# A hybrid S5 and RG-LRU block: the LRU stage in program order on three engines, its fill in 48 units of unsplit float32

## The chip, the cores and the metric

The kernel runs on one core of one Trainium2 chip. The metric is device time in microseconds, the median of the runs shown. TensorE (PE in the rows) multiplies, VectorE (DVE), ScalarE (ACT) and GpSimd (POOL) work elementwise, and SyncE (SP) issues the DMAs in one queue.

## What is computed

One layer with 2048 latent tokens and 256 context tokens, 1024 channels, all in float32. The mixer's input projection gives 512 channels to S5 and 512 to the RG-LRU; what follows bears on the change (cut from the reference).

```python
y_s5_lat = s5_glu(ys_lat[0] + ys_lat[1] + ys_lat[2], ...)      # y = gelu(y); y * sigmoid(y @ w_glu + b_glu)
...
xc = centred_depthwise_conv(xr, lru_conv_w, lru_conv_b)        # 4 taps
for d, reverse in enumerate((False, True)):
    r = sigmoid(block_diag(xc, w_rg[d], b_rg[d]))
    i = sigmoid(block_diag(xc, w_ig[d], b_ig[d]))
    log_a = -LRU_C * r * softplus(-lam)
    a, b = exp(log_a), sqrt(-expm1(2 * log_a)) * (i * xc)
    h_d = linear_scan(a, b, h0, reverse)                       # context first, then latent
...
y_lru_lat = from_col_major(h_0 + h_1, rows) * gelu(gr_lat)
out_lat = concatenate([y_s5_lat, y_lru_lat]) @ w_out
x = x + gt1 * rms_norm(out_lat, g_post_mix)                    # then a SwiGLU FFN
```

## The kernel before

`run` calls `front` (norm, input projection, S5 tables), `mix` (S5 scans, with the rest of the input projection as a fill for TensorE), `mix2` and `mix3` (the LRU stage) and `ffn`. The FFN's function begins with the LRU half of the output projection (`tile_out`, L1199 to L1212, tiles `oy`, `ogy`, `fpg`), which reads the S5 half of the output from DRAM (`OSD`) and the gated LRU output (`YLRU`) once all four channel groups are there.

A matrix product is mostly done in three parts: `split` (L59, L62) makes a float32r high part on ScalarE and a float32r low part on VectorE of each operand, and `mm3` (L70 to L72) or `mm3r` (L1028 to L1030) issues three matmuls. S5's own products (L774, L805, L812) and one sum over partitions (L1143) use float32 tiles as they are.

The LRU stage works on four groups `m` of 128 channels, with 2307 columns each (256 context, 3 of padding, 2048 latent). For each group `conv` loads the inputs and the gate weights, runs four passes on VectorE (L921, L923) and splits the result into five pieces of at most 512 columns. For each of two directions, `gates` (L938) computes r and i, 2 x 5 products of three matmuls, with a Sigmoid each, and multiplies i by the conv's result (L941). `decay` (L950, L951, L955, L956) runs Tanh, Exp and two half Squares on ScalarE and two products on VectorE. `scans` (L960, L961, L946) takes a Sqrt on ScalarE, a product and two scans on VectorE. The sum of both directions (L1004) times the gate that is loaded from `GGD` (L1002, L1006) is stored to `YLRU` (L1007). A group's gates are issued inside the iteration of the group ahead of it.

Beside it a fill runs that needs TensorE most: `glu`, eight blocks of 256 columns with 48 matmuls each, and `out_s5`, the S5 half of the output projection, 16 row tiles with two halves of 512 columns and 12 matmuls each; both split their inputs and use PSUM tiles `pgl`. What the fill is worth is written out by hand: the LRU generator yields a number of microseconds owed, and `run` (in `mix`) takes fill steps until it is paid (`DECAY_FILL`, `GATES_FILL`). Only ScalarE's order is the program's own (`manual_schedule`); the order on the other engines and in SP's queue is chosen by the framework's planner. What is left of the fill follows in `mix3`.

Of the kernel before, what the change touches and what calls it, by code (L numbers as in the profile page):

```python
# [18 lines left out]
D = 1024  # L19
# [7 lines left out]
T = 8  # L27
# [18 lines left out]
class Hybrid:  # L46
# [104 lines left out]
    S5_FILL, CONV_FILL, DECAY_FILL, GATES_FILL = 3.9, 0.1, 2.0, (0, 2, 2, 2)  # L151
# [32 lines left out]
    def mix(self):  # L184
# [31 lines left out]
        def rest():  # L216
            with ExitStack() as es:
                yield from self.glu(es)
            with ExitStack() as es:
                yield from self.out_s5(es)  # L220

        fill = rest()
        self.mm = (run, lru, fill, aes, bes)

    def mix2(self):
        run, lru, fill, aes, bes = self.mm

        with self.tc.manual_schedule(engines={self.nc.scalar.engine}):
            run(lru, fill)

    def mix3(self):
        run, lru, fill, aes, bes = self.mm
# [640 lines left out]
    def lru(self, es, bes):  # L873


# [27 lines left out]
        def conv(m):  # L903
# [7 lines left out]
            wh, wl = (p.tile([128, 4, 128], F32R, name=nm, bufs=2) for nm in ("lwh", "lwl"))  # L911
# [5 lines left out]
            self.split(wh, wl, wr)  # L917
# [6 lines left out]
            parts = []  # L924
            for j, (c0, n) in enumerate(CH):
                xh, xl = (p.tile([128, n], F32R, name=f"{nm}{j}") for nm in ("xh", "xl"))
                self.split(xh, xl, xc[:, c0:c0 + n])
                parts.append((xh, xl))
            return wh, wl, parts, xc

        def gates(m, d, wh, wl, parts, xc):
# [16 lines left out]
        def decay(m, d, r):  # L948
            t = pb.tile([128, XO + 1], F32, name="lt")
            nc.scalar.activation(t, r, AF.Tanh, scale=ccol[:, d * 4 + m:d * 4 + m + 1])  # L950
            nc.scalar.activation(r, r, AF.Exp, scale=ncol[:, d * 4 + m:d * 4 + m + 1])  # L951
            for h in halves:
                s = pb.tile([128, H], F32, name="lsq", bufs=2)
                sq = s[:, :h.stop - h.start]
                nc.scalar.activation(sq, r[:, h], AF.Square)  # L955
                v.scalar_tensor_tensor(t[:, h], sq, 1.0, t[:, h], op0=ADD, op1=MUL)  # L956
            return t

        def scans(d, r, i_, t):
            nc.scalar.activation(t, t, AF.Sqrt)  # L960
# [8 lines left out]
        turned = lambda q: q[:, LAT:XO].rearrange("p (c t r) -> p t r c", c=8, t=T)  # L969
        self.wgraw = p2.tile([128, XO + 1], F32, name="xc")[:, :4 * 512].rearrange("p (k f) -> p k f", k=4)  # L970
        nc.sync.dma_start(self.wgraw, A["s5_w_glu"][0].rearrange("(k p) f -> p k f", p=128))
        x = conv(0)
# [3 lines left out]
        yield self.CONV_FILL  # L976
        ri = []
        for d in range(2):
            yield from gates(0, d, *x)
            ri.append(self.rit)  # L980
        for m in range(4):
            ts = [decay(m, d, ri[d][0]) for d in range(2)]
            if m == 3:
# [27 lines left out]
            ri = nxt  # L1011

# [19 lines left out]
    def glu(self, es):  # L1032
# [5 lines left out]
        wg = []  # L1038
        for k in range(4):
            wh, wl = p.tile([128, 512], F32R, name=f"wgh{k}"), p.tile([128, 512], F32R, name=f"wgl{k}")  # L1040
            self.split(wh, wl, self.wgraw[:, k])
            wg.append((wh, wl))
        W = 256

        def load(n):
            y = st.tile([128, 4, W], F32, name="gy", bufs=3)
            nc.sync.dma_start(y, self.YD[:, :, n])
            yh, yl = st.tile([128, 4, W], F32R, name="gyh"), st.tile([128, 4, W], F32R, name="gyl")
            self.split(yh, yl, y)
            return y, yh, yl  # L1050

        def end(n, y, z):
            nc.scalar.activation(z, z, AF.Sigmoid)
            v.tensor_tensor(z, z, y, op=MUL)
            nc.sync.dma_start(self.YS5[:, :, n * W:(n + 1) * W], z)


# [533 lines left out]
```

## Time and profile before

| | us |
|---|---|
| median of 3 runs (lowest, highest) | 2323.95 (2319.48, 2329.18) |
| the profiled execution, its own time | 2329.66 |
| its span, first to last instruction | 2327.9 |
| busy in the span: TensorE | 2101.6 (90%) |
| VectorE | 1714.1 (74%) |
| ScalarE | 994.3 (43%) |
| GpSimd | 808.7 (35%) |
| mean granted TensorE clock | 0.946 |

The busy time of an engine is the sum over its instructions; a busy TensorE is not one at its peak, since matmuls are pipelined and a record overlaps the next. The granted clock is the share of full speed that TensorE's throttle let through: 1.00 is 2.4 GHz, 0.50 is 1.2 GHz, and what lies between is a mean of both. "Idle before" is the time an engine stood still ahead of an instruction, with what ended it. The shares are means over stages with different limits, so a stage is read by its own windows.

### The profile page before, as it was taken

The page shows a single profiled execution, that of the slowest core. Times are in us where ns is not written, and L with a number is a line of the kernel's source. Part 1 is how long each engine was busy: PE and PEld are TensorE (multiplying, and loading weights), DVE is VectorE, ACT ScalarE, POOL GpSimd, SP SyncE. Part 2 cuts the span into 40 slices and gives each one's busy share as a digit, 9 for nine tenths or more (in the row PEclk, how much of TensorE's full clock was granted, in tenths as well). Part 3 has the DMA queues.
Part 4 walks back from the last instruction along what each step waited for, and adds up shares of the span by engine and source line. Part 5 has one row for each costly group of instructions (what it writes and reads, how often), then busy time and mean ns, then how long its engine had stood idle before and what let it go on. Part 6 is the DMA issues. An engine that isn't in the chain of part 4 may idle for free. (4 is left out here: it accounts for less than half of the span.)

```text
span 2327.9 us, 27391 instructions
## 1 busy us (share of the span) xinstructions
PE 2101.6 (90%) x9460; PEld 1662.1 (71%) x9460; DVE 1714.1 (74%) x2243; ACT 994.3 (43%) x1561; POOL 808.7 (35%) x478
## 2 busy tenths in 40 slices
PE   6599998897674899879999999999999999999987
PEld 1477865575564677658888887788888878888866
DVE  6985458999998748956777878977787763534768
ACT  4688412112777626763333334333333333232424
POOL 1431420440000003343335545656565511400682
PEclk8799999898886899889999999999999999999999
DMA  9577756765233377863443334544444375634663
GB/s 261 171 243 255 232 149 211 212 206 171 71 122 115 127 236 251 285 222 108 146 136 127 109 100 141 176 139 160 143 156 145 136 262 172 214 100 157 226 219 121
DMA packets 311627, 403.29 MB, mean 173 GB/s; under 512 B 60176, under 2 KB 222528, under 8 KB 309952
## 3 DMA queue, kind: packets, MB, share of 16 engines
q1 hardware_dynamic: 311360, 401.50, 53.2%
q8 instruction: 75, 1.23, 0.2%
q14 instruction: 64, 0.52, 0.1%
q0 software_dynamic: 128, 0.04, 0.0%
HBM read 269.33 MB, written 132.12 MB: 172 GB/s over the span
## 5 line engine op out<-in xcount | busy, mean ns | idle before, releaser
L70 PE MATMUL fp<-op,fws 128*128 128x512 f32 x1232 | 486.9, 396 | 8.2 <-ACT op L59 7.5
L71 PE MATMUL fp<-op,fws 128*128 128x512 f32 x1232 | 486.4, 395 | 3.6 <-DVE op L62 2.4
L72 PE MATMUL fp<-op,fws 128*128 128x512 f32 x1232 | 485.3, 394 | 0.0
L70 PEld LDWEIGHTS fp<-op,fws 128*128 128x128 f32 x1232 | 233.7, 190 | 62.5 <-ACT op L59 9.1
L71 PEld LDWEIGHTS fp<-op,fws 128*128 128x128 f32 x1232 | 233.0, 189 | 58.9 <-DVE op L62 5.0
L72 PEld LDWEIGHTS fp<-op,fws 128*128 128x128 f32 x1232 | 233.1, 189 | 51.8
L1029 PE MATMUL po<-gw,ga 128*128 128x512 f32 x616 | 241.7, 394 | 9.4 <-DVE gw L62 9.4
L1028 PE MATMUL po<-gw,ga 128*128 128x512 f32 x616 | 241.6, 394 | 4.1 <-ACT ga L59 2.8
L1030 PE MATMUL po<-gw,ga 128*128 128x512 f32 x616 | 237.8, 391 | 1.5 <-DVE ga L62 1.5
L1348 POOL TENSOR_TENSOR fs<-fraw 128x512 f32<-128x512 f32 x44 | 68.4, 1554 | 484.0 <-DMA fraw<-in_w_ffn_in_dram 381.6
L62 DVE TENSOR_TENSOR fws<-fraw,fws 128x512 fp32r<-128x512 f32 x132 | 126.7, 961 | 56.5 <-ACT fws L59 55.6
L59 ACT ACTIVATE fws<-fraw 128x512 fp32r<-128x512 f32 x132 | 82.9, 629 | 147.0 <-PE fp L72 79.2
L1029 PEld LDWEIGHTS po<-gw,ga 128*128 128x128 f32 x616 | 117.2, 190 | 34.5 <-DVE gw L62 10.1
L1028 PEld LDWEIGHTS po<-gw,ga 128*128 128x128 f32 x616 | 117.3, 190 | 29.3 <-ACT ga L59 3.2
L1030 PEld LDWEIGHTS po<-gw,ga 128*128 128x128 f32 x616 | 116.2, 189 | 26.7 <-DVE ga L62 2.4
L62 DVE TENSOR_TENSOR fws<-fs,fws 128x512 fp32r<-128x512 f32 x132 | 118.1, 895 | 8.1 <-ACT fws L59 6.3
L59 ACT ACTIVATE fws<-fs 128x512 fp32r<-128x512 f32 x132 | 82.5, 626 | 93.2 <-PE fp L72 92.2
L62 DVE TENSOR_TENSOR ga<-gys,ga 128x1024 fp32r<-128x1024 f32 (+2 forms) x88 | 113.8, 1299 | 10.8 <-ACT ga L59 10.8
L71 PE MATMUL pu<-ht,winh 128*128 128x512 f32 (+1 forms) x256 | 100.8, 394 | 10.9 <-DVE ht L62 10.9
L70 PE MATMUL pu<-ht,winh 128*128 128x512 f32 (+1 forms) x256 | 102.3, 404 | 6.7 <-ACT ut L416 3.4
L62 DVE TENSOR_TENSOR gw<-gch,gw 128x512 fp32r<-128x512 f32 x44 | 51.6, 1172 | 71.5 <-ACT gw L59 71.5
L62 DVE TENSOR_TENSOR gw<-graw,gw 128x512 fp32r<-128x512 f32 x44 | 37.1, 843 | 88.7 <-ACT gw L59 85.4
(532 smaller groups left out, 4751.3 us busy)
## 6 DMA issues: line engine op xcount, KB each, us to landing
fraw<-in_w_ffn_in_dram SPq DMA_DIRECT2D x88, 512.0 KB, 4.4
graw<-in_w_ffn_out_dram SPq DMA_DIRECT2D x99, 256.0 KB, 3.6
gys<-S SPq DMA_DIRECT2D x44, 512.0 KB, 4.0
A<-faf SPq DMA_DIRECT2D x33, 512.0 KB, 2.6
S<-ost SPq DMA_DIRECT2D x33, 512.0 KB, 3.0
alw<-in_w_ada_dram SPq DMA_DIRECT2D x24, 512.0 KB, 5.0
ost<-A SPq DMA_DIRECT2D x22, 512.0 KB, 5.1
gys<-A SPq DMA_DIRECT2D x22, 512.0 KB, 5.0
```

The lines of the kernel that those rows point to most:

```text
L59: self.nc.scalar.activation(hi, src, AF.Identity)
L62: (eng or self.nc.vector).tensor_tensor(lo, src, hi.bitcast(F32), op=SUB)
L70: mm(ps, wh, xh, start=first, stop=False)
L71: mm(ps, wh, xl, start=False, stop=False)
L72: mm(ps, wl, xh, start=False, stop=last)
L1028: mm(ps, xh, wh, start=first, stop=False)
L1029: mm(ps, xh, wl, start=False, stop=False)
L1030: mm(ps, xl, wh, start=False, stop=last)
L1348: g.tensor_tensor(s[0], a21, a22, op=ADD)
```

## The change

`mix2` puts TensorE, ScalarE and VectorE in program order for the whole LRU stage. The LRU generator now yields a kind of fill, "g" or "o", and a count of units. A "g" unit is half a GLU block (2 x 4 matmuls of 256 columns into one PSUM tile), an "o" unit is one half of an output row tile (4 matmuls of 512 columns). Both use float32 operands without a split. There are 16 of the one and 32 of the other, 48 in all; four and three "g" units stand ahead of the gates of group 0, then 11 units go with each of groups 0 to 2 and seven with group 3, "g" units only where ScalarE's functions are Sigmoid and Tanh. A unit's eviction from PSUM is issued behind the matmuls of the next unit: two Sigmoids with the bias inside, or one copy, all on ScalarE.

In the LRU code the loads are apart from the conv, `parts` holds the splits and stands between the decay products and the Sqrt, the products of i with the conv's result stand ahead of the next conv, and the gating of a group (`gated`) is put off into the iteration of the next one. The sum of both directions goes into the conv's buffer. The GLU weights and the first four blocks of `w_out` are loaded into tiles of their own when the stage begins; before, the former came ahead of the conv of group 0 and the latter in group 1, and both were split.

```diff
     def mix2(self):
-        run, lru, fill, aes, bes = self.mm
-
-        with self.tc.manual_schedule(engines={self.nc.scalar.engine}):
-            run(lru, fill)
+        lru, aes, bes = self.mm
+        self.fes = ExitStack()
+        fill = {}
+
+
+        nc = self.nc
+        with self.tc.manual_schedule(engines={nc.tensor.engine, nc.scalar.engine, nc.vector.engine}):
+            for kind, n in lru:
+                if not fill:
+                    fill = self.lru_fill(self.fes)
+                for _ in range(n):
+                    next(fill[kind])
+            for f in fill.values():
+                for _ in f:
+                    pass
+            self.evict()
...
         self.wo = self.split_w_out(self.pool(self.wes, "wo_b", 1), self.woraw)
-        for _ in fill:
-            pass
+        self.fes.close()
         bes.close()
...
-        def conv(m):
+        def load(m):
...
-            self.split(wh, wl, wr)
+            return xs, wr
...
+        def parts(wr, xc):
+            wh, wl = (p.tile([128, 4, 128], F32R, name=nm, bufs=2) for nm in ("lwh", "lwl"))
+            self.split(wh, wl, wr)
...
-                yield self.GATES_FILL[m]
-            v.tensor_tensor(ri[1], ri[1], xc, op=MUL)
-            self.rit = ri
+            return ri
...
-            nc.scalar.activation(t, t, AF.Sqrt)
             v.tensor_tensor(i_, i_, t, op=MUL)
...
-        self.wgraw = p2.tile([128, XO + 1], F32, name="xc")[:, :4 * 512].rearrange("p (k f) -> p k f", k=4)
-        nc.sync.dma_start(self.wgraw, A["s5_w_glu"][0].rearrange("(k p) f -> p k f", p=128))
...
+        def gated(m, y, gg):
+            gv = gg.rearrange("p (t r c) -> p t r c", t=T, c=8)
+            v.tensor_tensor(gv, y[:, LAT:XO].rearrange("p (c t r) -> p t r c", c=8, t=T), gv, op=MUL)
+            nc.sync.dma_start(self.YLRU[:, m, :], gg)
...
+        yield "g", 4
+        xs, wr = load(1)
+        ri, old = [gates(0, 0, *x)], None
+        yield "g", 3
+        ri.append(gates(0, 1, *x))
         for m in range(4):
-            ts = [decay(m, d, ri[d][0]) for d in range(2)]
-            if m == 3:
+            for d in range(2):
+                v.tensor_tensor(ri[d][1], ri[d][1], xc, op=MUL)
+            if old:
+                gated(*old)
+            if m < 3:
+                xn = conv(m + 1, xs)
+            else:
 
                 raws = [p2.tile([128, XO + 1], F32, name="xc") for _ in range(2)]
                 self.woraw = [self.raw_w_out(raws[k // 2][:, k % 2 * D:(k % 2 + 1) * D], 4 + k) for k in range(4)]
-            else:
-                x = conv(m + 1)
-            yield self.DECAY_FILL
+            ts = [pb.tile([128, XO + 1], F32, name="lt") for _ in range(2)]
...
             for d in range(2):
-                scans(d, *ri[d], ts[d])
-            if m == 1:
-
-                raws = [ri[1][0][:, k * D:(k + 1) * D] for k in range(2)]
-                raws += [pb.tile([128, H], F32, name="lsq", bufs=2)[:, :D] for k in range(2)]
-                self.woraw = [self.raw_w_out(raws[k], k) for k in range(4)]
+                nc.scalar.activation(ts[d], ri[d][0], AF.Tanh, scale=ccol[:, d * 4 + m:d * 4 + m + 1])
+                if m < 3:
+                    yield "og"[d == 0], 1
+            for d in range(2):
+                r = ri[d][0]
+                nc.scalar.activation(r, r, AF.Exp, scale=ncol[:, d * 4 + m:d * 4 + m + 1])
+                yield "o", 1
+                for h in halves:
+                    s = pb.tile([128, H], F32, name="lsq", bufs=2)
+                    sq = s[:, :h.stop - h.start]
+                    nc.scalar.activation(sq, r[:, h], AF.Square)
+                    v.scalar_tensor_tensor(ts[d][:, h], sq, 1.0, ts[d][:, h], op0=ADD, op1=MUL)
+                yield "o", 1
+            if m < 3:
+                x = parts(wr, xn)
+                yield "o", 1
+            for d in range(2):
+                nc.scalar.activation(ts[d], ts[d], AF.Sqrt)
+                if d == 0 or m == 3:
+                    yield "o", 1
+            if m < 2:
+                xs, wr = load(m + 2)
             nxt = []
             if m < 3:
-                yield from gates(m + 1, 0, *x)
-                nxt.append(self.rit)
+                nxt.append(gates(m + 1, 0, *x))
+            scans(0, *ri[0], ts[0])
+            scans(1, *ri[1], ts[1])
             gg = ri[1][1][:, :SEQ]
             nc.sync.dma_start(gg, self.GGD[m])
-            y = ts[0]
-            v.tensor_tensor(y[:, LAT:XO], y[:, LAT:XO], ts[1][:, LAT:XO], op=ADD)
-            gv = gg.rearrange("p (t r c) -> p t r c", t=T, c=8)
-            v.tensor_tensor(gv, turned(y), gv, op=MUL)
-            nc.sync.dma_start(self.YLRU[:, m, :], gg)
+            y = xc if m < 3 else ts[0]
+            v.tensor_tensor(y[:, LAT:XO], ts[0][:, LAT:XO], ts[1][:, LAT:XO], op=ADD)
+            old = m, y, gg
+            yield ("g", 3) if m < 2 else ("o", 3) if m == 2 else ("o", 1)
             if m < 3:
-                yield from gates(m + 1, 1, *x)
-                nxt.append(self.rit)
+                nxt.append(gates(m + 1, 1, *x))
+                xc = xn
             ri = nxt
+        gated(*old)
...
+        wg = p.tile([128, 4, 512], F32, name="wg")
+        nc.sync.dma_start(wg, A["s5_w_glu"][0].rearrange("(k p) f -> p k f", p=128))
         W = 256
-
-        def load(n):
+        self.evict = lambda: None
+
+        def unit(end):
+            self.evict()
+            self.evict = end
...
+        gy = [load_g(n) for n in range(2)]
+        wo = [self.raw_w_out(p.tile([128, D], F32, name=f"wo{k}"), k) for k in range(4)]
+
+        def glu():
+            for n in range(8):
+                if n < 6:
+                    gy.append(load_g(n + 2))
+                z = st.tile([128, 4, W], F32, name="gz")
+                for m0 in (0, 2):
+                    pg = ps.tile([128, 2, W], F32, name="pgl")
+                    for m in (m0, m0 + 1):
+                        for k in range(4):
+                            nc.tensor.matmul(pg[:, m - m0], wg[:, k, m * 128:(m + 1) * 128], gy[n][:, k],
+                                             start=k == 0, stop=k == 3)
+
+                    def end(n=n, m0=m0, pg=pg, z=z):
+                        for m in (m0, m0 + 1):
+                            nc.scalar.activation(z[:, m], pg[:, m - m0], AF.Sigmoid,
+                                                 bias=self.colsB[:, C_BGLU + m:C_BGLU + m + 1])
+                        if m0:
+                            v.tensor_tensor(z, z, gy[n], op=MUL)
+                            nc.sync.dma_start(self.YS5[:, :, n * W:(n + 1) * W], z)
+
+                    unit(end)
+                    yield
+
+        def out():
+            ys = [load_o(i) for i in range(2)]
+            for i in range(16):
+                if i < 14:
+                    ys.append(load_o(i + 2))
+                o = st.tile([128, D], F32, name="oso")
+                for h in range(2):
+                    cs = slice(h * 512, (h + 1) * 512)
+                    po = ps.tile([128, 512], F32, name="pgl")
+                    for k in range(4):
+                        nc.tensor.matmul(po, ys[i][:, k], wo[k][:, cs], start=k == 0, stop=k == 3)
+
+                    def end(i=i, h=h, o=o, po=po, cs=cs):
+                        nc.scalar.activation(o[:, cs], po, AF.Copy)
+                        if h:
+                            nc.sync.dma_start(self.OSD[i], o)
+
+                    unit(end)
+                    yield
+
+        return {"g": glu(), "o": out()}
```

## Rows read from the trace of the kernel before

**Rows 1.** Stretches: us, busy us (count) by engine, PEclk, DMA share, GB/s.

```profile
577.00:600.00 23.00, 20.59 (x108) 17.92 (x108) 20.68 (x34) 17.18 (x28) 0.33 (x6) 0.88 0.44 149
600.00:665.00 65.00, 40.26 (x233) 35.71 (x234) 61.33 (x48) 43.52 (x49) 0.89 (x6) 0.81 0.30 102
831.00:871.00 40.00, 37.91 (x167) 30.82 (x167) 10.83 (x16) 8.61 (x14) 5.07 (x4) 1.00 0.82 266
```

**Rows 2.** Timeline of ScalarE: start us, us, engine, line, operation, tiles.

```profile
599.35 2.23 ACT L950 ACTIVATE lt<-lr,lc 128x2308 f32<-128x2308 f32 x1
614.40 2.48 ACT L59 ACTIVATE xh<-xc 128x512 fp32r<-128x512 f32 x5
779.78 2.24 ACT L950 ACTIVATE lt<-lr,lc 128x2308 f32<-128x2308 f32 x1
```

**Rows 3.** Timeline of SP's DMA queue, end of the LRU work.

```profile
830.08 0.32 SPq L1007 DMA_DIRECT2D YLRU<-li  x1
839.01 0.53 SPq L1201 DMA_DIRECT2D ogy<-YLRU  x1
```

**Rows 4.** Timeline of TensorE, where the next stage begins.

```profile
870.99 0.39 PE L1028 MATMUL fpg<-woh,oyh 128*128 128x512 f32 x1
871.22 0.39 PE L1029 MATMUL fpg<-wol,oyh 128*128 128x512 f32 x1
```

**Rows 5.** Tile pgl: ns min/median/max, first and last start us.

```profile
L70 PE MATMUL pgl<-gyh,wgh x128: 276/283/583, 577.7 to 719.8; 128*128 128x256 f32 x128
```

**Rows 6.** Groups of VectorE, 566 to 872 us: busy us, mean ns, idle.

```profile
L1073 DVE TENSOR_SCALAR gz<-pgl,colsB 128x256 f32<-128x256 f32 x32 | 14.5, 476 | 2.0 <-PE pgl L72 2.0
L1098 DVE COPY oso<-pgl 128x512 f32<-128x512 f32 x16 | 11.0, 686 | 20.3 <-PE pgl L1030 13.0 <-DMA OSD<-oso 7.3
L62 DVE TENSOR_TENSOR gyl<-gy,gyh 128x1024 fp32r<-128x1024 f32 x8 | 9.8, 1222 | 1.2 <-ACT gyh L59 1.2
L941 DVE TENSOR_TENSOR li<-li,xc 128x2308 f32<-128x2308 f32 x8 | 20.4, 2556 | 5.7 <-ACT li L938 5.7
L1006 DVE TENSOR_TENSOR li<-lt,li 128x2048 f32<-128x2048 f32 x4 | 15.7, 3916 | 1.2 <-DMA li<-GGD 1.2
L921 DVE TENSOR_SCALAR xc<-xs,colsB 128x2307 f32<-128x2307 f32 x4 | 5.9, 1478 | 0.8 <-DMA xs<-XRD 0.7
L923 DVE SCALAR_TENSOR_TENSOR xc<-xs,colsB,xc 128x2307 f32<-128x2307 f32 x12 | 31.4, 2617 | 0.1
L956 DVE SCALAR_TENSOR_TENSOR lt<-lsq,lt 128x1154 f32<-128x1154 f32 x16 | 21.3, 1356 | 13.5 <-ACT lsq L955 13.4
L946 DVE TENSOR_TENSOR_SCAN lt<-lr,lt,li 128x2048 f32<-128x2048 f32 x8 | 35.6, 4466 | 0.0
L1004 DVE TENSOR_TENSOR lt<-lt 128x2048 f32<-128x2048 f32 x4 | 9.1, 2286 | 0.0
```

**Rows 7.** Groups of ScalarE, 566 to 872 us, the same columns.

```profile
L938 ACT ACTIVATE lr<-pg,colsB 128x512 f32<-128x512 f32 x32 | 22.0, 688 | 12.2 <-PE pg L72 12.2
L938 ACT ACTIVATE lr<-pg,colsB 128x260 f32<-128x260 f32 x8 | 3.8, 477 | 4.3 <-PE pg L72 4.3
L955 ACT ACTIVATE lsq<-lr 128x1154 f32<-128x1154 f32 x16 | 17.8, 1157 | 0.2
L960 ACT ACT_TABLE_LOAD x4 | 5.1, 1283 | 0.1
L1101 ACT ACTIVATE oso<-pgl 128x512 f32<-128x512 f32 x16 | 9.5, 596 | 42.3 <-PE pgl L1030 31.9 <-DMA OSD<-oso 10.3
```

**Rows 8.** Timeline of TensorE, runs of float32 matmuls.

```profile
559.10 1.13 PE L805 MATMUL py<-u,md 128*128 128x256 f32 x4
395.79 1.12 PE L1143 MATMUL py<-g,ones 128*128 128x512 f32 x2
```

**Rows 9.** Tile li: loads of GGD, issue to landing.

```profile
DMA to landing us min/median/max: 4.6/4.7/5.1
```

**Rows 10.** Waits of ScalarE, 735 to 872 us: total, times, longest.

```profile
ACT oso L1101 <- PE pgl L1030: 31.9, 9, 7.3
```

More of the change, by code (lines that the diff above doesn't have):

```diff
@@ L214, in mix @@
             next(lru)
[L216 to L223, printed above, removed]
-    def mix2(self):
-        run, lru, fill, aes, bes = self.mm
-        with self.tc.manual_schedule(engines={self.nc.scalar.engine}):
-            run(lru, fill)
+        self.mm = (lru, aes, bes)
+    def mix2(self):
+        lru, aes, bes = self.mm
[12 more added lines that the diff above has]
+            self.evict()
     def mix3(self):
-        run, lru, fill, aes, bes = self.mm
+        lru, aes, bes = self.mm
         aes.close()
         self.wo = self.split_w_out(self.pool(self.wes, "wo_b", 1), self.woraw)
-        for _ in fill:
-            pass
+        self.fes.close()
         bes.close()
@@ L927, in conv, with gates @@
                 self.split(xh, xl, xc[:, c0:c0 + n])
-                parts.append((xh, xl))
-            return wh, wl, parts, xc
-        def gates(m, d, wh, wl, parts, xc):
+                ps_.append((xh, xl))
+            return wh, wl, ps_
+        def gates(m, d, wh, wl, parts):
             ri = [(pb.tile([128, XO + 1], F32, name=nm, bufs=1) if (2 * m + d) % 3 == 2 else
@@ L946, in lru @@
         scan = lambda o, a, b, x0: v.tensor_tensor_scan(o, a, b, x0, op0=MUL, op1=ADD)
[L948 to L957, printed above, removed]
         def scans(d, r, i_, t):
-            nc.scalar.activation(t, t, AF.Sqrt)
             v.tensor_tensor(i_, i_, t, op=MUL)
@@ L967, in scans @@
                 scan(t[:, XO - 1:LAT - 1:-1], r[:, XO - 1:LAT - 1:-1], i_[:, XO - 1:LAT - 1:-1], t[:, 0:1])
-        turned = lambda q: q[:, LAT:XO].rearrange("p (c t r) -> p t r c", c=8, t=T)
-        self.wgraw = p2.tile([128, XO + 1], F32, name="xc")[:, :4 * 512].rearrange("p (k f) -> p k f", k=4)
-        nc.sync.dma_start(self.wgraw, A["s5_w_glu"][0].rearrange("(k p) f -> p k f", p=128))
-        x = conv(0)
+        def gated(m, y, gg):
+            gv = gg.rearrange("p (t r c) -> p t r c", t=T, c=8)
+            v.tensor_tensor(gv, y[:, LAT:XO].rearrange("p (c t r) -> p t r c", c=8, t=T), gv, op=MUL)
+            nc.sync.dma_start(self.YLRU[:, m, :], gg)
+        xs, wr = load(0)
+        xc = conv(0, xs)
+        x = parts(wr, xc)
         yield None
@@ L1046, in load, with load_g @@
+        def unit(end):
+            self.evict()
+            self.evict = end
+        def load_g(n):
             y = st.tile([128, 4, W], F32, name="gy", bufs=3)
             nc.sync.dma_start(y, self.YD[:, :, n])
[L1048 to L1055, printed above, removed]
@@ L1059, in glu @@
-        nxt, last = load(0), None
-        yield 0.1
-        for n in range(8):
-            y, yh, yl = nxt
-            nxt = load(n + 1) if n < 7 else None
-            z = st.tile([128, 4, W], F32, name="gz")
-            for m in range(4):
-                if m % 2 == 0:
-                    pgs = ps.tile([128, 2, W], F32, name="pgl")
-                pg = pgs[:, m % 2]
-                ms = slice(m * 128, (m + 1) * 128)
-                for k in range(4):
-                    self.mm3(pg, wg[k][0][:, ms], wg[k][1][:, ms], yh[:, k], yl[:, k], k == 0, k == 3)
-                b = self.colsB[:, C_BGLU + m:C_BGLU + m + 1]
-                v.tensor_scalar(z[:, m], pg, b, None, op0=ADD)
-            if last:
-                end(*last)
-            last = n, y, z
-            yield 5.2
@@ L1078, in glu @@
-        end(*last)
-    def out_s5(self, es):
-        nc, v = self.nc, self.nc.vector
-        wop = self.pool(es, "wo_a", 1, side="right")
-        p = self.pool(es, "osp", 2, side="right")
-        ps = self.pool(es, "osps", 4, side="right", space=PSUM)
-        wo = self.split_w_out(wop, self.woraw)
-        yield 10.0
-        def load(i):
-            y = p.tile([128, 4, 128], F32, name="osy")
-            nc.sync.dma_start(y, self.YS5[:, :, i * 128:(i + 1) * 128])
-            yh, yl = p.tile([128, 4, 128], F32R, name="osyh"), p.tile([128, 4, 128], F32R, name="osyl")
-            self.split(yh, yl, y)
-            return yh, yl
-        def end(o, i, h, po):
-            cs = slice(h * 512, (h + 1) * 512)
-            if h:
-                v.tensor_copy(o[:, cs], po)
-                nc.sync.dma_start(self.OSD[i], o)
-            else:
-                nc.scalar.activation(o[:, cs], po, AF.Copy)
-        nxt, last = load(0), None
-        for i in range(16):
-            yh, yl = nxt
-            nxt = load(i + 1) if i < 15 else None
-            o = p.tile([128, D], F32, name="oso")
-            for h in range(2):
-                cs = slice(h * 512, (h + 1) * 512)
-                po = ps.tile([128, 512], F32, name="pgl")
-                for k in range(4):
-                    self.mm3r(po, yh[:, k], yl[:, k], wo[k][0][:, cs], wo[k][1][:, cs], k == 0, k == 3)
-                if last:
-                    end(*last)
-                last = o, i, h, po
-                yield 2.6
-        end(*last)
@@ new lines, in load_g, with load_o @@
+            return y
+        def load_o(i):
+            y = st.tile([128, 4, 128], F32, name="osy", bufs=4)
+            nc.sync.dma_start(y, self.YS5[:, :, i * 128:(i + 1) * 128])
+            return y
+        gy = [load_g(n) for n in range(2)]
[20 more added lines that the diff above has]
+                    yield
```

19 lines of the change are left out of this document (5 added, 14 removed).

## The prediction

> **What bounds the kernel now.** I read the stretches of the stage first, then the busy groups of VectorE and ScalarE in it, then four moments in the timelines. The chain that ended last lies wholly behind the stage (it begins at 1876 us), so it says nothing here; what counts is when the next stage, the LRU half of the output with the name fpg, can begin. In [rows 1] VectorE is busy for 61.3 of 65 us in the first whole channel group, while TensorE has 40.3 us and a mean clock of 0.81; after 831 us VectorE has 10.8 of 40 us and TensorE 37.9. So the stage has two parts: up to about 831 us VectorE's work sets the pace, and behind it 40 us in which TensorE only works off what is left of the S5 half of the output. The moments in [rows 2 to 4] give the same: the first tanh of group 0 starts at 599.35, that of group 3 at 779.78, so a group takes 60.1 us; the gated output of group 3 goes to DRAM at 830.08, and fpg starts only at 870.99, right behind the last S5 output. The first GLU matmul started at 577.7 [rows 5].
>
> **What is removed.** On VectorE, the bias adds behind the GLU, 14.5 us, half of the S5 output's copies, 11.0, the low parts of the GLU's input, 9.8 [rows 6], and three smaller kinds of split. ScalarE loses the high parts and takes the bias inside the Sigmoid, 32 of 256 columns (0.48 each, by the 260-column form) and 16 more copies of 0.60 [rows 7]. None of that is added to the sum by itself: it decides which engine is late in the walk below.
>
> **What TensorE pays.** A float32 matmul stands in the trace as two instructions. Four of 256 columns last 1.13 us from the first start to the last end, two of 512 columns 1.12 [rows 8]. A record outlasts the distance to the next start: 0.39 against 0.23 in [rows 4], so 0.16 of each figure is the drain. The first of a run waits 0.11 for its weights (an estimate: 1.13 - 0.16 = 0.97 = 0.11 + 4 x 0.215, and with the same two numbers 2 x 0.43 + 0.11 + 0.16 = 1.13, which the row of 512 columns gives). So a code matmul costs 0.43 at 256 columns, 0.86 at 512; a GLU unit (8 of 256) and an output unit (4 of 512) cost 3.45 each, and 48 units 165 us at full clock. The three-part form at 0.23 a piece would be 12 x 0.23 = 2.8 for an output unit: the change makes TensorE's own work longer by over a fifth. The gates of one direction stay as they are: 24 x 0.23 plus 6 of 260 columns at about half, 6.2 us.
>
> **The start.** The seven GLU units before group 0 are now ahead of its gates, in TensorE's order: 7 x 3.45 + 2 x 6.2 = 36.6. The GLU weights, 1 MB, now ask for their place in SP's queue just ahead of the first GLU input; between nothing (they leave while S5 is still being stored) and 4.7 us (the 1 MB load of GGD, from issue to landing [rows 9]) I take 1.3, so units start at 579. The four w_out blocks, 2 MB, and the next xs follow behind and are needed 40 us later: nothing. The clock was 0.88 in the first 23 us, a quarter of it at 1.2 GHz [rows 1]: 2.5 us lost. With the last Sigmoid, 0.7, the first tanh starts at 579 + 36.6 + 2.5 + 0.7 = 618.8, 19 us later than now.
>
> **The groups.** Per group TensorE has 11 units and two gates, 38 + 12.4 = 50.4. Group 0 takes 52: that, and 1.6 in which the gates wait for ScalarE's table load (1.28 [rows 7]). In groups 1 and 2 VectorE starts with the previous group's output: from the last Sigmoid, 2.56 (li x xc) + 3.92 (gating) + 9.33 (conv, 1.48 + 3 x 2.62) + 1.22 (a GLU product, the size of a split of 1024 columns) = 17.0, and only then the first decay product, 1.36 [rows 6]. ScalarE has its third Square ready to go at 15.7 but both lsq buffers are full until 18.4, and the fourth until 19.7. Behind it: Square to 20.9, the conv splits 3.1 (2.48 for the five pieces [rows 2] and 0.6 for the weights), evictions, table load and Sqrt (the size of the tanh, about 2.1) to 28.6, the second Sqrt 31.3, table load 32.6, ten Sigmoids at TensorE's pace to 38. Then three units, 10.4, and the other gates, 6.2, and a Sigmoid: 55. TensorE idles some 4 us in it. VectorE's two scan rows, 2 x (2.56 + 0.7 + 4.47), and the sum of both, 2.29, run from 28.6 to 46 beside the units: hidden, by 8 us. If the units' cover went, this path would still end before 55. So the groups take 52 + 55 + 55 = 162, and group 3 starts at 780.8, almost where it starts now.
>
> **The end.** Group 3 has no gates and no conv. ScalarE: two tanh 4.4, table 1.3, two Exp 4.4, four Squares 4.6, table 1.3, Sqrt 2.1, some evictions 1.8, about 20.5 with the wait for the last decay product. VectorE: 15.4 for two directions, to 36; the gate's load is issued then and takes 4.7 [rows 9], over the sum's 2.29; gating 3.92: 45. The trace has 50.3 for the same stretch, 779.78 to 830.08, with other work between; these are the bounds. From the store to fpg the load of the stored rows was issued 8.9 later, behind other DMAs [rows 3]; with load and split between 10 and 15, I take 11. TensorE has worked off the units by then, so fpg starts at 780.8 + 56 = 836.8, on a clock that has fallen: 2.5 more. Against 870.99 that is 31.7 us earlier, and the next stage follows as it did.
>
> The profiled execution took 2329.66 us (span 2327.9), 5.7 over the median of the runs: 2329.66 - 31.7 = 2298.0, and from the median, 2323.95 - 31.7 = **2292 us**.
>
> **Costed at nothing.** That y lies in xc, that the load of xs and the gate weights is apart from the conv, and the one unit behind group 3 (its eviction is done long before the gating ends). The input loads of the output units stand two tiles, four units or 14 us, ahead; a 1 MB load takes 4.7 [rows 9], so they cover. If SP holds them behind the load of GGD, which waits for the last scan, the units behind that stop, then the gates of direction 1, then the next tanh. Bounds: 0 and 5 us a group.
>
> **Rivals.**
> A. *The cadence stays.* The units stand in ScalarE's and VectorE's way as the splits did, or SP delays their inputs, and a group takes 60.1 as now [rows 2]. For it: the group's path has only 8 us of slack on VectorE. Against: the work removed from VectorE [rows 6]. Then 618.8 + 180.4 + 56 + 2.5 = 857.7, 13.3 gained: 2311.
> B. *TensorE alone counts.* The wait for the lsq buffers doesn't show and a group takes 50.4: 828.3, or 2281.
> C. *Taking turns, slower than before.* With three engines in program order, a unit's eviction waits in ScalarE's queue for TensorE, and tanh, Exp and Sqrt wait behind it. Place: the seven evictions between tanh and Sqrt. If every unit were waited for, a group would be 38 of units, 24.5 of ScalarE's own functions, 8 of evictions and 13.8 of gates: 84, the start of fpg at 930, the time 2383. It decides from 64.6 a group, (870.99 - 2.5 - 56 - 618.8) / 3, so from a wait of about 1 us at each of 11 units. For it: ScalarE waited 31.9 us for S5 output matmuls in the last third of the stage, in nine waits [rows 10]. Against: the eviction of a unit is issued behind the matmuls of the next, and four banks let TensorE run on; in the walk it is 1.5 to 3 us ahead at each.
> The Trainium skill's page "TensorE: Matmul & The Clock Gate" (Architectural detail) has ScalarE and VectorE as strict FIFOs, and that speaks for C; the nine waits agree with it.
> D. *The clock.* While TensorE had 40 of 65 us to do, its clock was 0.81 [rows 1]. If the idle pieces of the new order held it there, 50.4 would be 62 and a group about 66: 2328, no change. Against: the new groups leave 4 us idle of 55, and at 95% busy the clock was 1.00 [rows 1].
> The Trainium skill's page "TensorE: Matmul & The Clock Gate" (HAM oscillation) says that bursts broken by waits start each time on the slow clock, which speaks against so finely cut an order; by it the time would be D's, by the row of 831 to 871 us the forecast's.
>
> **How the numbers follow.** Chances: the walk 0.61, A 0.14, B 0.09, C 0.08, D 0.08. The range reaches from B with the two cold starts left out and its DMA wait at nothing, 2281 - 5 - 1.3 = 2274, to A with 3 for the weights' load, 2314: what is left out is C and most of D. A measurement of this kernel can tell about 0.5%, 11.6 us, from no change, so faster means under 2312. The walk and B are faster, and 0.09 of A's 0.14: 0.79. The rest of A and D: 0.13. Slower is C: 0.08.
>
> **What would show it.** Right: units of about 3.45 us from first to last start; the first tanh near 619; three distances of 52 to 55 between the tanh of successive groups; third Squares idle behind decay products; fpg near 837, with TensorE idle for some 25 us before it; the stage behind it as long as now. Wrong: tanh of groups 60 apart or more; ScalarE waiting long for pgl; units over 4 us; a stretch in the groups with a clock near 0.8; DMA as what units wait for.

## The result and the profile after

| us | before | after |
|---|---|---|
| median (lowest, highest), 9 runs each | 2320.5 (2312.59, 2330.99) | 2297.74 (2294.23, 2311.28) |
| ratio of the times, 95% interval | | 0.9900 (0.9883 to 0.9916) |
| the profiled execution, its own time | 2329.66 | 2294.62 |
| its span | 2327.9 | 2292.8 |
| mean granted TensorE clock | 0.946 | 0.957 |

The change makes the kernel 1.0% faster, 23 us, with an interval of 19.5 to 27. The prediction put what can be told from no change at 0.5%. The forecast was 2292 in a range of 2274 to 2314.

The two profiled executions differ by 35 us, and that is more than the change is worth. The next stages begin 27 us earlier, as shown below; the rest is the last stage (tile `po`), which took 437 us in the one profile and 428 in the other. In the seven further profiles of this study it took between 428 and 436, whatever was edited in the LRU stage, so nothing ties it to the change.

The busy times of the page show where not to look. Against the table ahead of the prediction, VectorE lost 50 us of work and ScalarE 11, and TensorE gained 8, but the gain can't be read from these sums:

```profile
PE 2109.9 (92%) x9204; PEld 1626.7 (71%) x9204; DVE 1664.5 (73%) x2163; ACT 983.7 (43%) x1569; POOL 811.2 (35%) x478
```

What counts is when the LRU stage ends. These are its stretches in the kernel after, to be held against [rows 1] (us, then busy us and count for TensorE, its weight loads, VectorE, ScalarE and GpSimd, then granted clock, DMA share, GB/s). They are cut at the moments of the new order: seven GLU units and the first gates, the groups 0, 1 and 2, the units beside group 3, the bare end, the next stage.

```profile
579.00:619.00 40.00, 40.00 (x178) 34.34 (x179) 6.92 (x9) 18.88 (x34) 0.00 (x0) 0.95 0.52 167
619.00:669.00 50.00, 50.00 (x181) 33.04 (x180) 42.55 (x26) 41.74 (x55) 0.69 (x4) 1.00 0.43 137
669.00:724.00 55.00, 51.82 (x181) 34.09 (x180) 46.50 (x26) 42.00 (x54) 0.79 (x5) 0.97 0.41 139
724.00:779.00 55.00, 51.81 (x156) 29.32 (x155) 45.44 (x25) 41.68 (x53) 0.10 (x1) 0.97 0.32 110
779.00:807.00 28.00, 27.69 (x64) 11.58 (x62) 20.30 (x13) 27.63 (x27) 0.00 (x0) 1.00 0.47 169
807.00:840.00 33.00, 0.00 (x0) 0.00 (x0) 17.11 (x6) 0.86 (x2) 4.04 (x4) 0.58 0.58 183
840.00:944.00 104.00, 99.38 (x435) 79.54 (x436) 89.52 (x172) 71.13 (x129) 35.38 (x16) 0.94 0.77 260
```

Before, TensorE had 40 of 65 us to do in a group, at a clock of 0.81, and 40 us of leftover work behind the stage. Now it is full in the groups (50 of 50, 52 of 55, clock 0.97 to 1.00), and nothing is left behind group 3: it stands still from 807 to 840, waiting for the LRU output.

The moments, in us, for all kernels of this study ("units": first and last start of their matmuls; tanh: first start in group 0 and in group 3; the three distances are those between the first tanh of successive groups; "store": issue of group 3's store to `YLRU`; `fpg`: first matmul of the next stage; `fp`: first matmul of the FFN behind it):

```
kernel               units          tanh 0  distances          tanh 3  store   fpg    fp
before               577.7 - 870.8  599.4   65.5  61.5  53.5   779.8   830.1   871.0   982.8
after                579.0 - 806.3  618.6   50.2  55.3  55.2   779.3   826.7   840.4   955.8
e5_unsplit_only      576.8 - 872.0  607.8   58.1  56.5  65.0   787.3   837.4   872.1   985.6
e4_fill_last         718.4 - 923.8  588.1   40.2  46.5  46.2   721.0   767.1   923.9  1039.3
e3_two_banks         576.9 - 809.2  616.0   50.6  53.7  53.7   774.0   822.9   836.5   951.9
e1_squares_in_xs     580.8 - 799.2  619.8   50.2  51.1  51.1   772.2   819.6   833.1   947.0
e2_wo_late           573.8 - 800.2  613.2   50.2  55.3  55.2   773.9   818.0   831.6   947.5
e6_shift             578.4 - 818.2  607.1   51.6  55.1  56.4   770.2   819.7   834.5   950.9
e7_all               581.5 - 812.0  611.3   51.5  51.2  51.2   765.1   810.3   826.3   940.5
```

One of the four runs of `e5_unsplit_only` took 9190.55 us, four times the others, and stands in no figure below.

From tanh 0 to tanh 3 a group now takes 53.6 on average instead of 60.1, but the first tanh comes 19 later, so group 3 starts when it did (779.3 against 779.8). The LRU output is stored 3.3 us earlier, no more. The gain is behind it: before, the next stage waited for the units until 871.0; now it starts 13.7 us behind the store.

The timeline of ScalarE shows a group in the kernel after (start us, us, line, operation, tiles, and in brackets the idle time before it with what ended it):

```profile
618.59 2.23 ACT L993 ACTIVATE lt<-lr,lc 128x2308 f32<-128x2308 f32 x1
...
646.80 0.69 ACT L947 ACTIVATE lr<-pg,colsB 128x512 f32<-128x512 f32 x1
...
655.11 0.84 ACT L1094 ACTIVATE gz<-pgl,colsB 128x256 f32<-128x256 f32 x2 [2.25 <-PE pgl L1089]
658.57 0.84 ACT L1094 ACTIVATE gz<-pgl,colsB 128x256 f32<-128x256 f32 x2 [2.62 <-PE pgl L1089]
...
668.80 2.23 ACT L993 ACTIVATE lt<-lr,lc 128x2308 f32<-128x2308 f32 x1
...
687.34 2.38 ACT L1003 ACTIVATE lsq<-lr 128x1154 f32<-128x1154 f32 x2 [3.55 <-DVE lt L1004]
...
699.55 1.28 ACT L947 ACT_TABLE_LOAD   x1
700.84 0.69 ACT L947 ACTIVATE lr<-pg,colsB 128x512 f32<-128x512 f32 x1
...
792.75 2.22 ACT L1003 ACTIVATE lsq<-lr 128x1154 f32<-128x1154 f32 x2
794.86 3.89 ACT L59 ACTIVATE woh<-xc 128x1024 fp32r<-128x1024 f32 x4
...
839.70 0.63 ACT L59 ACTIVATE oyh<-ogy 128x512 fp32r<-128x512 f32 x1 [32.14 <-DMA ogy<-YLRU]
```

Two GLU units are evicted 3.46 us apart: that is the price of a unit. The third and fourth Square of group 1 wait 3.55 for VectorE's decay product. In group 3 four splits of `w_out` stand behind the last Square, 3.89 us, ahead of the Sqrt.

The tile `pgl` in the kernel after (ns min/median/max, first and last start), and at its end who waited for it:

```profile
L1089 PE MATMUL pgl<-gy,wg x256: 377/379/763, 579.0 to 726.5; 128*128 128x256 f32 x128
L1113 PE MATMUL pgl<-wo,osy x256: 592/592/697, 621.2 to 806.3; 128*128 128x512 f32 x128
...
  DVE gz L1097: 27.2, 3
  ACT gz L1094: 18.4, 8
  ACT oso L1116: 5.4, 3
```

ScalarE waited 31.9 us for S5 output matmuls in the last third of the old stage [rows 10]; over the whole of the new one it is 5.4. Its 18.4 for GLU units lie at the start and in the three units at the end of a group, where the walk of the prediction has TensorE set the pace.

### The profile page after: what moved, and what is told of

Read it like the earlier page. It is cut to its first block, busy times and chain, and to the rows that moved or that the text cites. A ratio compares the mean times of both kernels' runs of the same rounds, so it can differ in the third digit from the quotient of the medians.

```text
span 2292.8 us, 26775 instructions
## 1 busy us (share of the span) xinstructions
PE 2109.9 (92%) x9204; PEld 1626.7 (71%) x9204; DVE 1664.5 (73%) x2163; ACT 983.7 (43%) x1569; POOL 811.2 (35%) x478
## 5 line engine op out<-in xcount | busy, mean ns | idle before, releaser
L62 DVE TENSOR_TENSOR ga<-gys,ga 128x1024 fp32r<-128x1024 f32 (+2 forms) x88 | 120.6, 1375 | 14.7 <-ACT ga L59 14.4
L1113 PE MATMUL pgl<-wo,osy 128*128 128x512 f32 x256 | 111.2, 593 | 0.2 <-ACT oso L1116 0.2
L72 PE MATMUL pu<-ht,winl 128*128 128x512 f32 (+1 forms) x256 | 99.6, 389 | 0.0
```

Of the source, the lines that this page charges most:

```text
L62: (eng or self.nc.vector).tensor_tensor(lo, src, hi.bitcast(F32), op=SUB)
L72: mm(ps, wl, xh, start=False, stop=last)
L1113: nc.tensor.matmul(po, ys[i][:, k], wo[k][:, cs], start=k == 0, stop=k == 3)
```

## The experiments

The theory to be tested is the walk of the prediction: the order lets TensorE take the units beside the groups, and a group is then set by single, nameable waits on ScalarE and VectorE. Its rivals were that the units' simpler form alone brought the gain, that the wait for the Square buffers was cover and not path, and that taking turns held the groups at 55. The ratios below set times against the kernel before; the intervals of e1, e2 and e6 overlap with that of the kernel after, so what each of them adds to it is read from the profiles, one execution each.

**e5_unsplit_only: the kernel before, with the operands unsplit.** With the splits their buffers go: the weights are loaded straight into tiles of their own, and the output units' inputs have four buffers instead of two. The order is still the planner's, and the fill steps and evictions stay.

```diff
-            self.split(yh, yl, y)
-            return y, yh, yl
+            return y
...
-                    self.mm3(pg, wg[k][0][:, ms], wg[k][1][:, ms], yh[:, k], yl[:, k], k == 0, k == 3)
+                    nc.tensor.matmul(pg, wg[:, k, ms], y[:, k], start=k == 0, stop=k == 3)
...
-                    self.mm3r(po, yh[:, k], yl[:, k], wo[k][0][:, cs], wo[k][1][:, cs], k == 0, k == 3)
+                    nc.tensor.matmul(po, y[:, k], wo[k][:, cs], start=k == 0, stop=k == 3)
```

> The kernel before with one part of the change alone: GLU and S5 half of the output in float32 matmuls without splits; the order, the steps of the fill and the evictions stay as they were. Theory (the order and the place of the units carry the gain): VectorE loses 28 us of low parts, so the LRU work ends between 803 and 831 us, but about 15 output units are still left then, as in the kernel before, and at 3.45 us instead of 2.72 they take 52 us: fpg begins between 855 and 883, the time is 2310 to 2335, no change or a small gain. Rival (dropping the splits is what gains): fpg near 840 and 2297, as in the changed kernel.

Measured: 2322.48, 2331.6 and 2333.25 us, against a median of 2321.18 of the kernel before on the same chip, ratio 1.005 (1.003 to 1.0071): no gain, and by the median about 0.5% slower, though VectorE has less to do. The LRU work did not end between 803 and 831 as expected, but at 837.4. `fpg` starts 1.1 us later than before; where the rest lies, the profile doesn't show, since it is of the fastest of these runs. Why nothing is gained, it does, in the columns of above:

```profile
600.00:665.00 65.00, 40.95 (x163) 32.26 (x161) 51.35 (x37) 43.02 (x51) 0.79 (x5) 0.79 0.29 98
837.00:872.00 35.00, 30.81 (x71) 13.52 (x72) 6.18 (x9) 4.24 (x7) 4.97 (x4) 1.00 0.78 255
```

VectorE went from 61.3 to 51.4 of 65 us [rows 1], and no engine took the room: TensorE still has 41 us at a clock of 0.79, and still 35 us of units behind the store. Less work on the busiest engine brought nothing while the order stayed the planner's. The other half, the new order with the three-part splits, wasn't tried. So what is shown is that the unsplit form alone does not bring the gain; whether the order alone would is open.

**e4_fill_last: the new order, with all 48 units behind group 3.**

```diff
             for kind, n in lru:
                 if not fill:
                     fill = self.lru_fill(self.fes)
-                for _ in range(n):
-                    next(fill[kind])
```

> The changed kernel with no unit beside the groups: all 48 stand behind group 3. It shows what the LRU chain costs alone. Theory (group 0 is set by TensorE's units, groups 1 and 2 by the chain VectorE - Squares - Sqrt - gates - units - gates): without units a group takes 46 to 48 us, set by VectorE's 45, the first tanh starts near 591, that of group 3 near 731, and fpg comes behind 165 us of units near 905, so the time is about 2360. If the units cost the groups nothing, the groups would stay at 50 and 55 us. If the chain's waits alone set the 55, it would stay for groups 1 and 2.

Measured: 2383.76 us (one run). The bare groups take 40.2, 46.5 and 46.2: the 46 to 48 of the expectation in groups 1 and 2, but not in group 0, where VectorE has 2.5 us of work ahead of the conv instead of 8.7. So the units and their evictions cost 10 us in group 0 and 9 in the others, where they hold TensorE for 38: about three quarters is hidden. The tail is hardly shortened (721.0 to 767.1, 46.1 us against 47.4), which points away from the seven units beside it. `fpg` came 19 later than expected: the 16 GLU units, in program order ahead of the output units, took from 718.4 to 814.2. TensorE stood twice among them:

```profile
745.96 9.83 PE L1087 MATMUL pgl<-gy,wg 128*128 128x256 f32 x32 [13.61 <-ACT gz L1092]
777.55 37.01 PE L1087 MATMUL pgl<-gy,wg 128*128 128x256 f32 x160 [21.77 <-DMA gy<-YD]
```

The first evictions stand in ScalarE's row behind the Sqrt of group 3. The longer wait is for the next GLU inputs, whose loads were issued from 769.20 on, after VectorE, behind the gating of group 3, had begun at 766.96 to multiply the first blocks. The 32 output units behind them took 3.43 each (814.4 to 923.8), with nothing beside them.

**e3_two_banks: two PSUM banks for the units instead of four.**

```diff
-        ps = self.pool(es, "gps", 4, side="right", space=PSUM)
+        ps = self.pool(es, "gps", 2, side="right", space=PSUM)
```

> The changed kernel with two PSUM banks for the units instead of four, so that TensorE can be one unit ahead of ScalarE's evictions and not three. Theory (TensorE's lead is what keeps evictions from blocking tanh, Exp and Sqrt): TensorE stands still in the stretches in which ScalarE runs its own functions, the evictions behind them come late, and a group takes 57 to 62 us; fpg 10 to 25 us later. Turning rival C on: if the lead decides everything, a group comes near 65 and more, and the time near that of the kernel before. If the lead is not used, groups stay at 50 and 55.

Measured: 2299.57 us (one run, no faster than the kernel after), groups of 50.6, 53.7 and 53.7. The expectation was wrong twice. The lead of three units over the evictions is worth nothing here, so the rival of taking turns falls with its price: with two banks TensorE's matmuls wait 2.6 us in all for evictions between 616 and 775. And with two banks groups 1 and 2 are 1.5 us *faster*. The timelines of TensorE in the gates of direction 0 show where, first in the kernel after:

```profile
698.01 0.39 PE L72 MATMUL pg<-xh,lwl 128*128 128x512 f32 x1
701.58 0.50 PE L70 MATMUL pg<-xh,lwh 128*128 128x512 f32 x1 [3.18 <-ACT lr L947]
...
703.25 0.63 PE L70 MATMUL pg<-xh,lwh 128*128 128x512 f32 x1
703.68 0.63 PE L71 MATMUL pg<-xl,lwh 128*128 128x512 f32 x1
...
756.89 0.50 PE L70 MATMUL pg<-xh,lwh 128*128 128x512 f32 x1 [3.19 <-ACT lr L947]
...
757.85 0.63 PE L70 MATMUL pg<-xh,lwh 128*128 128x512 f32 x1
758.28 0.63 PE L71 MATMUL pg<-xl,lwh 128*128 128x512 f32 x1
```

and then with two banks:

```profile
697.63 0.39 PE L72 MATMUL pg<-xh,lwl 128*128 128x512 f32 x1
699.46 0.50 PE L70 MATMUL pg<-xh,lwh 128*128 128x512 f32 x1 [1.44 <-ACT lr L947]
...
701.42 0.39 PE L72 MATMUL pg<-xh,lwl 128*128 128x512 f32 x1
701.65 0.39 PE L70 MATMUL pg<-xh,lwh 128*128 128x512 f32 x1
```

In both TensorE has filled the banks of the gates and stands until ScalarE, back from the Sqrt's table, takes the first Sigmoid. With four banks it comes there earlier and stands 3.18 us, and 3.19 in group 2; soon behind that, matmuls of 512 columns start 0.43 apart instead of 0.23. With two it stands 1.44, and the distance stays 0.23. The granted clock of these stretches in group 1, kernel after:

```profile
701.50:703.20 1.70, 1.62 (x6) 1.35 (x7) 1.70 (x1) 1.70 (x5) 0.00 (x0) 0.90 0.00 0
703.20:705.80 2.60, 2.60 (x7) 2.00 (x6) 2.60 (x2) 1.91 (x4) 0.00 (x0) 0.50 0.03 6
```

and with two banks:

```profile
700.70:703.40 2.70, 2.70 (x16) 2.36 (x15) 2.70 (x2) 2.70 (x6) 0.00 (x0) 1.00 0.02 6
```

So the longer pause is paid for a second time, by at least 2.6 us at 1.2 GHz. The Trainium skill's page "TensorE: Matmul & The Clock Gate" (HAM oscillation) has bursts behind waits start on the slow clock. The trace agrees in part: in the kernel after, the burst behind the 3.2 us pause began at full clock, 0.23 apart, and slowed 1.3 us later in group 1 and 0.6 in group 2; in the kernel of e6, below, it was slow from its start in both groups. The burst behind the shorter pause of two banks didn't slow, in group 1 or in group 2.

**e1_squares_in_xs: the wait for the Square buffers taken away.** The Squares of direction 1 in groups 0 to 2 go into the conv's input tile, which is free by then.

```diff
-                    s = pb.tile([128, H], F32, name="lsq", bufs=2)
-                    sq = s[:, :h.stop - h.start]
+                    if d and m < 3:
+                        sq = xs[:, h]
+                    else:
+                        s = pb.tile([128, H], F32, name="lsq", bufs=2)
+                        sq = s[:, :h.stop - h.start]
```

> The changed kernel with the Squares of the second direction in groups 0 to 2 written into the conv's input tile, which is free when the conv is done, so that they don't wait for the first decay products. Theory (that wait, 3.55 us in groups 1 and 2, is on the path): groups 1 and 2 take 52.5 instead of 55.2, group 0 stays at 50.2, fpg comes 5 us earlier, near 835. Rival (VectorE's row of conv, decay products and low parts is the path, and the Squares only wait beside it): the low parts end where they ended, groups stay at 55 within 1 us.

Measured: 2289.97 us (two runs) against 2321.18, ratio 0.9867 (0.9848 to 0.9887). Groups 1 and 2 take 51.1, 4.1 less. ScalarE's timeline in this kernel, group 1:

```profile
684.39 0.59 ACT L1119 ACTIVATE oso<-pgl 128x512 f32<-128x512 f32 x1
686.12 2.22 ACT L1006 ACTIVATE xs<-lr 128x1154 f32<-128x1154 f32 x2 [1.15 <-issue]
```

The Squares now start 1.7 us behind the start of the eviction ahead of them, against 4.1 before (683.20 and 687.34). The rest of the 4.1 lies in the gates: TensorE's pause there is 0.62 us in this kernel and the distance of matmuls stays 0.23. So the wait was on the path, as the prediction had it, and it drew the clock's price behind it; the groups came 1.4 under the 52.5 expected, about that price.

**e2_wo_late: the four splits of `w_out` issued behind the groups, in program order.**

```diff
             self.evict()
+            aes.close()
+            self.wo = self.split_w_out(self.pool(self.wes, "wo_b", 1), self.woraw)
...
-        aes.close()
-        self.wo = self.split_w_out(self.pool(self.wes, "wo_b", 1), self.woraw)
```

> The changed kernel with the splits of the last four w_out blocks written out behind the LRU work on ScalarE and VectorE, where the text of the program has them; in the changed kernel the planner put them between the last Squares and the first Sqrt of group 3 (3.89 us of ScalarE, 4.62 of VectorE). Theory (they lie on the path that ends the stage): the stretch from the tanh of group 3 to its store shrinks from 47.4 to between 43 and 44 us and fpg comes about 4 us earlier, near 836; the splits then run beside the store and the load of the stored rows. Rival (they only fill a wait for the decay products): the stretch stays at 47 and fpg at 840, or comes later by the splits.

Measured: 2290.77 us (two runs) against 2321.17, ratio 0.9864 (0.9816 to 0.9913). From tanh 3 to the store it takes 44.1 instead of 47.4. In the kernel after, these splits are written behind the block in program order, and the planner still placed them among ScalarE's and VectorE's instructions of group 3. ScalarE in this kernel goes on from the last Square to one eviction and the table:

```profile
787.33 2.23 ACT L1003 ACTIVATE lsq<-lr 128x1154 f32<-128x1154 f32 x2
789.93 0.60 ACT L1116 ACTIVATE oso<-pgl 128x512 f32<-128x512 f32 x1 [0.38 <-DMA OSD<-oso]
790.55 1.28 ACT L1010 ACT_TABLE_LOAD   x1
```

The units of this execution also began 5 us earlier than in the kernel after, at 573.8, which the edit doesn't touch; so 3.3 us is the edit's part, and the median of the two runs holds more than that.

**e6_shift: three GLU units moved from the start to the end of group 2, three output units of group 0 and three of group 2 to group 3.** In groups 0 and 3, where no unit follows the second tanh, the eviction still open is issued there. The units stay 48.

```diff
-        yield "g", 4
+        yield "g", 2
...
-        yield "g", 3
+        yield "g", 2
...
-            yield ("g", 3) if m < 2 else ("o", 3) if m == 2 else ("o", 1)
+            yield ("g", 3) if m < 3 else ("o", 8)
```

> The changed kernel with units moved from the start into the tail: two and two GLU units ahead of group 0's gates instead of four and three, four output units instead of seven beside group 0, three GLU units at the end of group 2, and the eight output units that are left behind the Sqrt of group 3, where TensorE stands still for 33 us. Theory (the start is TensorE's alone, 3.45 us a unit, and the tail has room): the first tanh at 608, group 0 in 42 to 47 us, groups 1 and 2 in 55 as before, fpg 13 to 18 us earlier than 840, the time near 2281. Rival (what is taken from the start comes back, since the GLU results are late for the output units): group 0 stays at 50 or ScalarE waits long for pgl, and no more than 5 us are gained.

Measured: 2289.0 us (4 runs) against 2321.17, ratio 0.9852 (0.9812 to 0.9892). The start gave what was expected: the first tanh at 607.1. Group 0 gave nothing: 51.6, with three units fewer in it. ScalarE's timeline of this kernel, from the tanh to the first Sigmoid of the next gates:

```profile
607.14 2.23 ACT L996 ACTIVATE lt<-lr,lc 128x2308 f32<-128x2308 f32 x1
...
635.28 0.69 ACT L950 ACTIVATE lr<-pg,colsB 128x512 f32<-128x512 f32 x1
```

That is 28.1 us, and 28.2 in the kernel after (618.59 to 646.80), where ScalarE has no idle time in between. So in group 0 two paths have nearly the same length: TensorE's units and gates, and ScalarE's own functions (here with three evictions fewer, but 0.96 of waiting for a decay product), then three units and the gates of direction 1. Shortening the one leaves the other. The 1.4 us that group 0 is longer than in the kernel after (51.6 against 50.2) lie behind that first Sigmoid, in the gates: with less to do TensorE stood for 4.08 us there (632.0 to 636.0), and its clock was low. The whole group, in the columns of above:

```profile
607.00:659.00 52.00, 45.23 (x160) 31.70 (x159) 42.90 (x26) 41.62 (x53) 0.69 (x4) 0.87 0.39 125
```

In the kernel after it is 1.00. From the first unit to `fpg` it is 256.1 us instead of 261.4, a gain of 5.3 where 13 to 18 were expected. The rival's numbers came, group 0 at 50 and about 5 us, but not its reason: ScalarE waited only 4.9 us for `pgl` from 605 to 660, in two waits.

**e7_all: the edits of e1, e2 and e6 together.**

> The three edits together: Squares in the conv's input tile, w_out splits behind the LRU work, units moved into the tail. Theory (each takes away its own piece of the path): 14 to 16 us from the start and group 0, 8 from groups 1 and 2, 4 from group 3, fpg between 811 and 816, the time 2268 to 2275. Rival (with the chain shorter TensorE's units, 165 us of them, and the gates, 50, become the bound): fpg not before 820.

Measured: 2279.85 us (6 runs) against 2321.17, ratio 0.9824 (0.9792 to 0.9856): faster than the kernel before by 1.8%, where the kernel after has 0.9900 (0.9883 to 0.9916). Groups take 51.5, 51.2 and 51.2, and `fpg` starts at 826.3, where 811 to 816 was expected, with a time of 2268 to 2275. The rival (not before 820) was right in groups 1 and 2: there TensorE has become the bound, with hardly any idle time. The windows of these groups in this kernel:

```profile
662.00:713.00 51.00, 50.38 (x181) 32.98 (x180) 46.47 (x26) 41.80 (x55) 0.79 (x5) 1.00 0.45 154
713.00:765.00 52.00, 51.37 (x185) 33.70 (x185) 46.48 (x26) 42.81 (x57) 0.10 (x1) 1.00 0.36 127
```

Group 0 is not TensorE's: it has 40 us of units and gates and takes 51.5, as in e6, with the clock at 0.90. In all, 48 units at 3.45 and eight gates at 6.2 are 215 us of TensorE's work, and the units lie between 581.5 and 812.0, in 230. What is left beyond these 15 us is the end: 45.2 from tanh 3 to the store and 16.0 from there to `fpg`.

## Why the prediction was right, point by point

- *The mechanism.* TensorE's leftover behind the stage goes beside the groups: right, and shown by the windows and by e5 and e4. `fpg` was put at 836.8, 34.2 us earlier, and came at 840.4, 30.6 earlier. With the cold clock behind it the gain was put at 31.7; to be set against that is the start of the FFN, 27.0 earlier in the profiled pair. The medians give 23 (19.5 to 27), so the forecast of the gain was too high. The end and the cold clock, below, are 4.7 of the difference; the other 4 lie between the profiled pair and the medians and stay open.
- *A unit costs 3.45.* Measured 3.46 for a GLU unit in a group and 3.43 for an output unit in e4.
- *The start.* Units at 579.0 (predicted 579), the first tanh at 618.6 (618.8). Right.
- *Group 0, 52 by TensorE and a table load.* Measured 50.2. TensorE is full, as walked (50.4); the 1.6 of waiting for the table load did not come. What the walk didn't have is ScalarE's own row as a second path of nearly the same length, which e6 shows.
- *Groups 1 and 2, 55 by VectorE's row and the Square buffers.* Measured 55.3 and 55.2. From the last Sigmoid to the first decay product VectorE took 16.9 us (predicted 17.0), the wait is 3.55, and e1 shows that it is on the path. VectorE in group 1:

```profile
668.95 2.56 DVE L982 TENSOR_TENSOR li<-li,xc 128x2308 f32<-128x2308 f32 x1 [4.48 <-ACT li L947]
...
685.89 5.28 DVE L1004 SCALAR_TENSOR_TENSOR lt<-lsq,lt 128x1154 f32<-128x1154 f32 x4
```

  What the walk lacked is the slow clock in the gates, some 1.5 us by e3; so its other terms were together too long by about as much, which of them wasn't measured, and the agreement to 0.3 us is partly luck.
- *The end, 45 + 11.* Measured 47.4 + 13.7. This is the mis-sized term, by 5.1 us. The first part, 2.4, is the `w_out` splits: the prediction's list for group 3 has none, and e2 gives 3.3 for them, so the rest of the list was 0.9 too long. The second is the way from the store to `fpg`, for which 11 was taken from between 10 and 15. In SP's queue of the kernel after, three loads of the FFN's weights stand ahead of the LRU output:

```profile
826.74 0.32 SPq L967 DMA_DIRECT2D YLRU<-li  x1
827.11 4.87 SPq L1335 DMA_DIRECT2D fraw<-in_w_ffn_in_dram  x3
832.03 1.58 SPq L1205 DMA_DIRECT2D oy<-OSD  x1
833.70 0.53 SPq L1207 DMA_DIRECT2D ogy<-YLRU  x1
```

  From store to load it is 7.0 us (8.9 before [rows 3]), and 6.0 more to the split. The 4.87 us are no measure of what moving those loads would bring: a store to `YLRU` takes 4.5 to 4.9 from issue to landing in this kernel, and the load reads what it wrote. It wasn't tried.
- *The cold clock at `fpg`, 2.5.* The next stage, from `fpg` to `fp`, takes 115.4 instead of 111.8, 3.6 more. Right in kind, and 1.1 larger.
- *The rivals.* A (60.1 a group) didn't come. B (50.4) came only with e1's edit: 51.1. C falls with e3: even with two banks the groups stay at 54 and under. D (0.81 in the groups) didn't come, but its mechanism did, once in each of groups 1 and 2, for 2.6 us or more.

Together: group sum 160.7 against 162, the start as foreseen, the end 5.1 longer, and so `fpg` 3.6 later than predicted. The time of 2297.74 lies 5.7 over the forecast. That it lies no further is in part luck: the forecast starts from 2323.95, the median of three runs, and over nine runs the kernel before has 2320.5; from there the same 31.7 would have given 2288.8.

## What to carry to other kernels

When an engine has slack in a stage and leftover work behind it, look for who decides its order before cutting the work: here, less work in the old order brought nothing, and the same work in a written order closed the gap (whether the old operands in the new order would have done it too is not shown). Then walk one period of the new order with every engine's own row and every buffer; when two rows come out nearly equal, an edit to one alone may buy nothing, as in group 0 of e6. And what is written behind a stage can still be placed inside it, if only part of the program is in program order.

## What the hardware showed that was not expected

- In the gates of groups 1 and 2 a pause of TensorE of 3.2 us was followed by at least 2.6 us on the slow clock all six times (kernel after, e2, e6); pauses of 1.4 us (e3) and 0.6 us (e1, e7) in the same place were not, in six cases. Fewer PSUM banks gave the shorter pause and the faster group (53.7 against 55.2).
- The `po` stage takes between 428 and 437 us in profiles of kernels that have it unchanged. A difference of two profiled executions is not the gain; here it overstates it by half (35 against 23).
